# A 64 KB store of zeros on ScalarE's queue, beside the first load of a log-softmax backward kernel

## Chip, cores and metric

The kernel runs on one core of a Trainium2 chip. The metric is the device time of one execution in microseconds (us). Runs of one kernel mostly agree within 0.3%.

## The reference

```python
def reference(y, dy):                       # both (8, 1024, 8192) float32
    softmax_x = np.exp(y)
    sum_dy = np.sum(dy, axis=-1, keepdims=True)
    return (dy - softmax_x * sum_dy).astype(np.float32)
```

Two arrays of 268 MB are read and one is written: 805 MB for very little arithmetic.

## The kernel before

The 8192 rows are handled in 32 groups of 256; a partition holds two rows of a group side by side, 64 KB. VectorE sums dy (with the sign turned), ScalarE takes the exponential of y in place, VectorE computes `e * s + d` into the dy tile, and the dy tile is stored. All transfers are issued from one queue, SyncE's (SP).

```python
    def load_dy(g):
        dy_t = dyp.tile([P, R * D], fp32, name="dy_t")          # 2 buffers of 64 KB a partition
        nc.sync.dma_start(out=dy_t[:], in_=dy_v[g])             # line 45
        s_t = stats.tile([P, R], fp32, name="s_t")
        nc.vector.tensor_reduce(...)                            # line 47
        return dy_t, s_t

    def load_y(g): ...      # two loads of 32 KB rows, line 60
    def compute(...): ...   # line 69: nc.scalar.activation; line 70: nc.vector.scalar_tensor_tensor
    def store(g, dy_t, parts=1): ...                            # line 77, on nc.sync

    cur = load_dy(0)
    for g in range(G):                                          # G = 32
        if g < G - 1:
            y_ts = load_y(g)
            compute(*cur, y_ts)
            nxt = load_dy(g + 1)
            if g < G - 2:
                store(g, cur[0])
                cur = nxt
            else:
                held, cur = cur, nxt
        else:
            ...             # last group: its compute, the held store, then the last store in two parts
```

## Time and profile before

| | before |
|---|---|
| time, median of the three runs known at the start | 1871.92 us (1868.21 to 1875.18) |
| span of the profiled execution | 1865.4 us |
| busy: VectorE (DVE), ScalarE (ACT) | 60%, 25% |
| bytes moved, mean rate | 805 MB, 432 GB/s |

The next fence is from the page of the kernel before: the row of DMA busy tenths in 40 equal slices, and the queue table (queue, packets, MB, share of sixteen engines' span).

```profile
DMA  9999999999999999999999999999999999999999
...
q1 hardware_dynamic: 18576, 805.31, 99.9%
```

The DMA engines never rest and no compute engine comes near that, so the DMA engines set the time.

The timeline of the head of the kernel before has the start, the duration, engine (SPq is SP's queue of issues), line and operation, and in brackets the engine's idle time before it and what ended that.

```profile
0.73 0.38 SPq L45 DMA_DIRECT2D dy_t<-in_dy_dram  x1
1.17 0.90 SPq L60 DMA_DIRECT2D y_t<-in_y_dram  x2
2.11 0.53 SPq L45 DMA_DIRECT2D dy_t<-in_dy_dram  x1
22.74 17.22 DVE L47 TENSOR_REDUCE s_t<-dy_t 128x2 f32<-128x16384 f32 x1 [22.74 <-DMA dy_t<-in_dy_dram]
32.42 7.12 ACT L69 ACTIVATE y_t<-y_t 128x4096 f32<-128x4096 f32 x2 [30.42 <-DMA y_t<-in_y_dram]
...
57.77 0.35 SPq L77 DMA_DIRECT2D out_dram<-dy_t  x1
...
113.31 0.34 SPq L77 DMA_DIRECT2D out_dram<-dy_t  x1
```

The four loads issued in the first 2.64 us hold 25 MB, some 58 us of DMA work. VectorE has nothing to do until 22.74 us and ScalarE nothing but its table load until 32.42 us. The first store follows at 57.77 us, close to where the four loads end.

The wait view for SP's queue before (who waited for whom, total us, times, longest):

```profile
SPq L77 <- DVE dy_t L70: 985.9, 32, 35.0
SPq L45 <- DMA out_dram<-dy_t: 742.0, 30, 25.6
```

Stores wait for VectorE and dy loads wait for a store to free their buffer. Since the engines are busy anyway, these waits cost nothing as they stand.

### The profile page before, as it was taken

Reading aid. Unit: us, or ns where it says so; the run is one execution under the profiler, and the core shown is the slowest. Engines: PE = TensorE matmul, PEld = TensorE weight load, DVE = VectorE, ACT = ScalarE, POOL = GpSimd, SP = SyncE. Lnnn points to the kernel's source line nnn. Section 1 sums busy time; section 2 is a strip of 40 time slices with the busy share of each in tenths; the row PEclk is TensorE's granted clock in tenths of the full one; section 3 lists DMA queues with packets and bytes.
Section 4 is the critical chain, followed back from the end, with each engine's and each line's share of the span. In section 5 each row is a group of like instructions: output and inputs, shape, how many; then the busy total and the mean of one; then the engine's idle time right before and its main releaser. Section 6 shows DMA issues by size and latency. Waiting matters only on the chain.

```text
span 1865.4 us, 712 instructions
## 1 busy us (share of the span) xinstructions
DVE 1119.2 (60%) x160; ACT 457.1 (25%) x129; POOL 0.2 (0%) x4
## 2 busy tenths in 40 slices
DVE  5675555755557555575555755657656576565664
ACT  2123321233212332123321233212332113331132
POOL 0000000000000000000000000000000000000000
DMA  9999999999999999999999999999999999999999
GB/s 427 416 434 431 443 433 422 435 437 436 427 433 431 440 430 434 431 429 441 433 437 425 433 442 431 434 425 436 438 434 433 428 434 437 437 431 430 429 435 396
DMA packets 18582, 805.36 MB, mean 432 GB/s; under 512 B 2064, under 2 KB 2064, under 8 KB 2064
## 3 DMA queue, kind: packets, MB, share of 16 engines
q1 hardware_dynamic: 18576, 805.31, 99.9%
q14 instruction: 6, 0.05, 0.0%
HBM read 536.87 MB, written 268.44 MB: 432 GB/s over the span
## 4 chain that ended last, share of the span: by engine, by line
DMA 74%; DVE 17%; ACT 6%; SPq 1%; issue 1%; DVEq 0%; ACTq 0%
DMA y_t<-in_y_dram 69%; DVE dy_t L70 15%; ACT y_t L69 6%; DMA dy_t<-in_dy_dram 3%; DVE s_t L47 2%; DMA out_dram<-dy_t 1%; SPq L60 1%; SPq L77 1%; DVEq L122 0%; ACTq L69 0%; DVEq L70 0%
## 5 line engine op out<-in xcount | busy, mean ns | idle before, releaser
L70 DVE SCALAR_TENSOR_TENSOR dy_t<-y_t,s_t,dy_t 128x4096 f32<-128x4096 f32 x128 | 568.1, 4481 | 490.3 <-ACT y_t L69 490.1
L69 ACT ACTIVATE y_t<-y_t 128x4096 f32<-128x4096 f32 x128 | 455.9, 3608 | 1375.6 <-DMA y_t<-in_y_dram 1375.6
L47 DVE TENSOR_REDUCE s_t<-dy_t 128x2 f32<-128x16384 f32 x32 | 551.0, 17220 | 232.1 <-DMA dy_t<-in_dy_dram 232.1
L69 ACT ACT_TABLE_LOAD x1 | 1.3, 1283 | 0.7 <-PEq L111 0.7
L111 POOL MEMSET const-bfloat16-1.0<- 128x1 bf16 x1 | 0.1, 102 | 0.0
L111 POOL MEMSET const-uint8-127<- 128x1 uint8 x1 | 0.1, 102 | 0.0
L111 POOL MEMSET const-float32-1.0<- 128x1 f32 x1 | 0.1, 99 | 0.0
L111 POOL MEMSET const-float32-0.0<- 128x1 f32 x1 | 0.1, 98 | 0.2 <-issue 0.2
## 6 DMA issues: line engine op xcount, KB each, us to landing
y_t<-in_y_dram SPq DMA_DIRECT2D x64, 4096.0 KB, 35.9
out_dram<-dy_t SPq DMA_DIRECT2D x2, 4096.0 KB, 22.6
dy_t<-in_dy_dram SPq DMA_DIRECT2D x32, 38.7
out_dram<-dy_t SPq DMA_DIRECT2D x31, 26.1
```

The lines of the kernel that those rows point to most:

```text
L47: nc.vector.tensor_reduce(out=s_t[:], in_=dy_t[:].rearrange("p (r d) -> p r d", r=R), axis=mybir.AxisListType.X, op=ALU.add, negate=True,)
L60: nc.sync.dma_start(out=y_t[:], in_=y_v[g][:, r * D : (r + 1) * D])
L69: nc.scalar.activation(e, e, EXP)
L70: nc.vector.scalar_tensor_tensor(out=d, in0=e, scalar=s_t[:, r : r + 1], in1=d, op0=ALU.mult, op1=ALU.add)
L77: nc.sync.dma_start(out=out_v[g][:, k * w : (k + 1) * w], in_=dy_t[:, k * w : (k + 1) * w])
L111: nc = _bacc.Bacc("TRN2", target_bir_lowering=False, num_devices=1)
```

## The change

The change adds one store on a second queue before anything else. It writes zeros into rows of the last group's output, which the last group's own store overwrites at the end. No reason comes with it; what it does is to have a write, and a second queue, in use from the start.

```diff
+    first_t = stats.tile([P, 128], fp32, name="first_t")
+    nc.vector.memset(first_t[:], 0.0)                                   # line 83
+    nc.scalar.dma_start(out=out_v[G - 1][:, :128], in_=first_t[:])      # line 84
+
     cur = load_dy(0)
```

## The prediction

> **What bounds the kernel now.** The DMA engines. In the row of slices their busy share is 9 tenths or more in all 40; the queue table puts 805.31 MB and 99.9% of sixteen engines' span on the one hardware queue (SP's), at a mean of 432 GB/s over 1865.4 us. VectorE is busy 60%, ScalarE 25%. In the timeline ScalarE starts on two neighbouring late groups at 1719.50 and 1777.57, so a group takes 58.1 us; it moves 25.17 MB, which is 433 GB/s. The time is bytes over a rate that hardly moves (slices from 396 to 443 GB/s), plus about 1 us before the first bytes and about 3 us after most of the last ones (the windows view has 295 GB/s in 1860 to 1862 us, 49 in the next two).
>
> **What the change adds.** It removes nothing.
> - A memset of 128x128 on VectorE. The four small memsets in the trace take 0.1 us each; I estimate 0.1 to 0.2 us. VectorE is idle until 22.74 us (timeline): free.
> - One DMA issue on ScalarE, some 0.4 us as on SP (0.33 to 0.53 us), beside the table load at 0.72 to 2.00 us. ScalarE has nothing else to do before 32.42 us: free.
> - 64 KB on the DMA engines, in 128 rows of 512 B. By bytes at 432 GB/s that is 0.15 us. The rows are small: the Trainium skill, "DMA: Bandwidth & Descriptors", section "Measured", lists 0.95 us of engine time for a 64 KB transfer (a load by another path, so an estimate of the upper end). The trace before holds no such data packet, so it neither agrees nor disagrees.
> - Probably one more semaphore condition on the last group's first store and one more queue in the final drain, both met some 1800 us earlier: below 0.1 us.
>
> **How much is on the critical path.** Only the DMA engine time. By 2.64 us SP has issued the first dy load, both y loads and the second dy load, 25 MB or 58 us of work, so what the small store takes from the engines delays everything behind it and arrives whole at the end: 0.15 to 1 us, 0.3 us as my figure, 0.02% of the time. Less, if the store slips in before the first load's bytes flow. The small store may itself land late, even 20 us, if its rows take turns with the first load's 64 KB rows; nobody waits for it. The order of work on SP should stay, since no other transfer depends on the new one until the last group.
>
> The three runs before spread over 7 us (1868.21 to 1875.18), far more than the effect; that spread sets my range.
>
> **Predicted:** 1872.2 us, 1866.5 to 1878.5 eight times in ten. Faster by over 2%: 0.01; within 2%: 0.97; slower by over 2%: 0.02.
>
> **What would show the steps right or wrong.**
> - The queue table gains a second hardware queue with 65.5 KB and far below 0.1%; the first stays at 805.31 MB and 99.8 to 99.9%.
> - A group stays at 58.1 us; the slices stay at 9s with some 430 GB/s.
> - The first reduction starts at 22.7 us plus at most 1 us; the last store is issued at most 1 us later than 1841.6 us.
> - In the wait view no new wait longer than 1 us appears on SP, ScalarE or VectorE.
>
> **What would make it wrong.** An early write to the output that makes later transfers wait for one another (new waits on SP, gaps in the DMA row); a reordering of SP's instructions; or a DMA rate that changes once two queues have been in use (another group period through the whole run). A gain over 2% would need more than 440 GB/s sustained, which only single slices of the trace show.

## The result, and the profile after

| | before | after |
|---|---|---|
| median of 6 runs | 1868.88 us | 1868.38 us |
| lowest to highest | 1867.29 to 1875.18 | 1867.66 to 1871.71 |
| profiled span | 1865.4 us | 1866.1 us |

The ratio is 0.9993, 95% interval 0.9977 to 1.0010: the same. A ratio is the mean time of one kernel's fast runs over that of the other's fast runs of the same rounds, so it is not quite the ratio of the medians quoted.

From the page of the kernel after, the DMA row, the queue table, and the issue line of the new store (KB, us from issue to landing):

```profile
DMA  9999999999999999999999999999999999999999
...
q1 hardware_dynamic: 18576, 805.31, 99.9%
q10 hardware_dynamic: 144, 0.07, 0.0%
...
out_dram<-first_t ACTq DMA_DIRECT2D x1, 64.0 KB, 22.9
```

(ACTq is ScalarE's queue of issues.) The old queue is untouched and a second one has 128 rows and 16 completion records of 4 B, one for each DMA engine. But those 64 KB took 22.9 us to land, that is, from issue until all of it was reported as done.

The timeline of the head after, with lines 83 and 84 new:

```profile
0.73 0.38 SPq L45 DMA_DIRECT2D dy_t<-in_dy_dram  x1
0.82 0.17 DVE L83 MEMSET first_t<- 128x128 f32 x1 [0.82 <-PEq L116]
1.02 0.41 ACTq L84 DMA_DIRECT2D out_dram<-first_t  x1
...
22.70 17.22 DVE L47 TENSOR_REDUCE s_t<-dy_t 128x2 f32<-128x16384 f32 x1 [21.71 <-DMA dy_t<-in_dy_dram]
32.39 7.12 ACT L69 ACTIVATE y_t<-y_t 128x4096 f32<-128x4096 f32 x2 [29.65 <-DMA y_t<-in_y_dram]
...
57.72 0.35 SPq L77 DMA_DIRECT2D out_dram<-dy_t  x1
...
113.53 0.34 SPq L77 DMA_DIRECT2D out_dram<-dy_t  x1
```

Every line shown of before has its counterpart within 0.3 us. ScalarE's table load alone moved by more: it starts at 1.46 us, 0.72 before, behind the issue of the new store. SP's wait view after:

```profile
SPq L77 <- DVE dy_t L70: 985.3, 32, 35.0
SPq L45 <- DMA out_dram<-dy_t: 743.3, 30, 25.7
```

No new wait appears on SP. ScalarE's wait view has one, that of its table load:

```profile
ACT L69 <- DVE first_t L83: 1.5, 1, 1.5
```

The trace also keeps each packet of the DMA engines. This is an excerpt of the records after (time since the first load's first packet, queue, bytes, duration), the sixteen engines mixed:

```
  3.491 q1    65536 B  2420 ns
  3.525 q1    65536 B  2418 ns
  5.404 q10     512 B    27 ns
  5.428 q1    65536 B  2418 ns
  5.449 q10     512 B    27 ns
  5.472 q1    65536 B  2418 ns
```

Each engine puts one 512 B row between two 64 KB rows and no more; one such place of the small row is called a turn here. The start of one round of 64 KB rows to the next is 2.415 us before (median start of the rounds 3.32 and 17.81 us, six rounds apart) and 2.438 us after (3.31 and 17.94 us). So one turn costs 23 ns, the eight turns that an engine owes cost some 0.2 us, and the store is finished only after eight of those rounds: each engine's first six small rows stand between 64 KB rows, the seventh after its last one, and the eighth behind the 4 B completion record of that load. That is my theory of the result: the store costs its turns, 0.2 us, and its late landing is harmless while nobody waits for it. The Trainium skill says of this, in "DMA: Bandwidth & Descriptors", section "Queues, rings and completion order", that an engine "round-robins between the queue rows it has work for, at *packet* granularity"; the records above agree, with one record, here one row, to a turn.

### The profile page after: what moved, and what is told of

It reads as the page before. It is cut to its first block, busy times and chain, and to the rows that moved or that the text cites. A ratio compares the mean times of both kernels' runs of the same rounds, so it can differ in the third digit from the quotient of the medians.

```text
span 1866.1 us, 714 instructions
## 1 busy us (share of the span) xinstructions
DVE 1119.4 (60%) x161; ACT 457.1 (24%) x129; POOL 0.2 (0%) x4
## 3 DMA queue, kind: packets, MB, share of 16 engines
q1 hardware_dynamic: 18576, 805.31, 99.9%
## 4 chain that ended last, share of the span: by engine, by line
DMA 74%; DVE 17%; ACT 6%; SPq 1%; issue 1%; DVEq 0%; ACTq 0%
DMA y_t<-in_y_dram 69%; DVE dy_t L70 15%; ACT y_t L69 6%; DMA dy_t<-in_dy_dram 3%; DVE s_t L47 2%; DMA out_dram<-dy_t 1%; SPq L60 1%; SPq L77 1%; DVEq L127 0%; ACTq L69 0%; DVEq L70 0%
## 6 DMA issues: line engine op xcount, KB each, us to landing
out_dram<-first_t ACTq DMA_DIRECT2D x1, 64.0 KB, 22.9
```

## The experiments

All kernels gave the right result. The edits are against the changed kernel, except in the two experiments that start from the kernel with small rows; "..." marks lines left out.

### The change again, and a null

The first repeats the changed kernel and the second is the kernel before against itself, five rounds each.

> The changed kernel once more, in five rounds. My theory: the store costs only its turns on the DMA engines, 8 rows of 27 ns per engine in the trace, 0.22 us, so the ratio to the kernel before is 1.0001 and no run of this length can see it: 0.999 to 1.001. Rival: opening a second hardware queue, or an early write, slows something for good; then the ratio is above 1.001 in every round.

> The kernel before against itself, five rounds: what a ratio of no change looks like here. Expected within 0.999 to 1.001, as wide as for the changed kernel.

| | median | ratio to before | 95% |
|---|---|---|---|
| change again | 1868.24 us | 0.9992 | 0.9978 to 1.0007 |
| before against itself | 1869.84 us | 1.0001 | 0.9985 to 1.0017 |

The null has an interval as wide as the change's, and both hold 1; the rival's 1.001 lies above that of the change (1.0007). An effect of 0.2 us (0.01%) can't be seen in time here; it must be made larger. The expected width of 0.1% was a little too narrow.

### The store 32 times larger, in small rows

```diff
-    nc.scalar.dma_start(out=out_v[G - 1][:, :128], in_=first_t[:])
+    nc.scalar.dma_start(
+        out=out_v[G - 1][:, :8192].rearrange("p (k c) -> p k c", c=256)[:, :, :128],
+        in_=first_t[:].unsqueeze(1).to_broadcast([P, 32, 128]),
+    )
```

> The store made 32 times larger in the same 512 B rows (2.10 MB, 256 rows per engine), one DMA. Turns theory: 256 x 27 ns = 6.9 us more engine time, all of it in the span: +6 to +9 us, ratio 1.003 to 1.005. The store takes one turn per row of the SP queue, 32 rows per engine in a group of 58 us, so it lands only after some 465 us. No new wait on SP. Rival 1 (bytes alone count): 2.10 MB at 432 GB/s, +4.9 us. Rival 2 (it hides in the head): +0 to 1 us, landing within some 30 us.

The median was 1878.06 us against 1868.92, ratio 1.0048 (1.0027 to 1.0069), so some +9 us. Landing and a wait were not as expected. The issue line of the early store, from this kernel's page:

```profile
out_dram<-first_t ACTq DMA_DIRECT2D x1, 2048.0 KB, 125.5
```

SP's wait view of this kernel:

```profile
SPq L77 <- DVE dy_t L70: 953.0, 31, 35.0
...
SPq L77 <- DMA out_dram<-first_t: 42.8, 1, 42.8
```

And from its timeline, VectorE's last work on the second group and that group's store:

```profile
106.45 8.88 DVE L70 SCALAR_TENSOR_TENSOR dy_t<-y_t,s_t,dy_t 128x4096 f32<-128x4096 f32 x2 [0.99 <-ACT y_t L69]
...
126.57 0.34 SPq L77 DMA_DIRECT2D out_dram<-dy_t  x1
```

The turns go as expected at first: by the packet records 32 rows an engine by 58 us. Then the second group's store, whose data are ready at 106.45 + 8.88 = 115.3 us, is held until 126.57 us, although it writes other rows (the 42.8 us count from SP's issue before; 11.2 of them come after the data are ready). SP's queue runs dry, and the other 187 rows of each engine flow back to back in 4.4 us, one every 23.5 ns; then the engines stand still for 1.3 us, until the first row of the next store. So the cost is some 6.0 us (from start to start) to 6.9 us (256 x 27 ns) of rows and 1.3 us of idle time, 7 to 8 of the 9 us. The rest is within the noise: the large rows alone took 1863.1 us of each engine in the profiled run before and 1868.1 us in that of the null. Hiding in the head (0 to 1 us) is far outside the interval (5.0 to 12.9 us). Bytes alone (4.9 us) is just outside, but inside once the 1.3 us of idle time are added; what speaks against it is the 6.0 to 6.9 us of the records.

Why it waits shows in the compiled program's listing of SP's instructions, here from the changed kernel (second column: line in the kernel):

```
8  L77 DMACopy out_dram<-dy_t 128x16384 [waits DMAHW4_49,DMAHW1_49,DVE_49]     after
8  L77 DMACopy out_dram<-dy_t 128x16384 [waits DMAHW3_49,DVE_49]               before
```

The listing itself is not kept with the runs, but the trace of the changed kernel agrees: the early store and the second group's store both raise semaphore 101, and SP waits for that one ahead of the latter. The program has eight completion counters for transfers (in the trace, semaphores 100 to 103 and 105 to 108), taken in turn. The early store has counter 1, and the transfer eight places later, the second group's store, shares it and so waits for it. That condition is in the changed kernel too: it is met at 23.9 us, some 90 us before the store that asks for it.

### The same bytes in 8 KB rows

```diff
-    first_t = stats.tile([P, 128], fp32, name="first_t")
+    first_t = stats.tile([P, 2048], fp32, name="first_t", bufs=1)
...
-    nc.scalar.dma_start(out=out_v[G - 1][:, :128], in_=first_t[:])
+    nc.scalar.dma_start(
+        out=out_v[G - 1][:, :8192].rearrange("p (k c) -> p k c", c=4096)[:, :, :2048],
+        in_=first_t[:].unsqueeze(1).to_broadcast([P, 2, 2048]),
+    )
```

> The same 2.10 MB in 8 KB rows (16 per engine), one DMA. Turns theory: some 0.30 us a row, 16 x 0.30 = 4.9 us more engine time and as much in the span, ratio 1.0026, about 2 us less than with the small rows; 16 turns behind eight 64 KB rows and eight 32 KB rows, so landing at some 35 us, thirteen times earlier than the small rows. Rival (cost is per byte and landing per byte): same time and same landing as with the small rows.

The median was 1873.95 us, against the same 1868.92: ratio 1.0020 (1.0003 to 1.0037), 3.7 us by the ratio and 5.0 by the medians. The store's issue line, from this kernel's page:

```profile
out_dram<-first_t ACTq DMA_DIRECT2D x1, 2048.0 KB, 35.8
```

The first reduction, from its timeline:

```profile
25.47 17.22 DVE L47 TENSOR_REDUCE s_t<-dy_t 128x2 f32<-128x16384 f32 x1 [22.48 <-DMA dy_t<-in_dy_dram]
```

It landed after 35.8 us, as the count of turns said, and its 8 KB rows took 309 ns each, 16 x 0.309 = 4.9 us an engine. The first reduction moved from 22.70 to 25.47 us, most of which is the seven turns taken ahead of the first load's completion records (7 x 0.309 = 2.2 us). Same bytes, another landing: landing goes by rows, cost by the time of the rows. For the cost that rests on the packet records, since the two intervals overlap.

### Small rows to the first group

```diff
-        out=out_v[G - 1][:, :8192].rearrange("p (k c) -> p k c", c=256)[:, :, :128],
+        out=out_v[0][:, :8192].rearrange("p (k c) -> p k c", c=256)[:, :, :128],
```

> The 2.10 MB in 512 B rows again, but to rows of the first group, whose real store is wanted at 57.7 us. Theory (the late landing was harmless only because nobody waits for it): now SP waits at its first store. By then 24 to 32 of 256 turns per engine are taken; the SP queue runs dry at about 60 us, and then the other 224 rows flow at 27 ns each, 6 us. So a new SP wait of some 8 to 10 us, the first store is issued at 66 to 69 us, landing at about 66 us, not 465, and the span is 2 to 6 us longer than with the same rows in the last group (+9 to +13 us against before). Rival (landing never matters, the engines are busy with something anyway): the same time as with the last group's rows.

The median was 1877.69 us, against 1869.55: ratio 1.0052 (1.0023 to 1.0081). From SP's wait view of this kernel:

```profile
SPq L77 <- DMA out_dram<-first_t: 65.2, 1, 65.2
```

And the first group's store, from its timeline:

```profile
68.05 0.35 SPq L77 DMA_DIRECT2D out_dram<-dy_t  x1
```

The first store moved from 57.72 to 68.05 us, as expected (the 65.2 us count from SP's issue before; VectorE is done at 58.0 us, so some 10 of them are new). But the time is that of the last group's rows, since those made a store wait too. The comparison of the two therefore decided nothing; what it shows is that a late landing is felt once someone waits for it. The records have the same 1.3 us in which all engines stand still, here at 67.6 us.

### Another partner on the counter

To tell the shared counter from a check of overlapping rows, the small-rows kernel got two more transfers between the early store and the second group.

```diff
-            nc.sync.dma_start(out=y_t[:], in_=y_v[g][:, r * D : (r + 1) * D])
+            h = D // 2 if g == 0 else D
+            for c in range(0, D, h):
+                nc.sync.dma_start(
+                    out=y_t[:, c : c + h], in_=y_v[g][:, r * D + c : r * D + c + h]
+                )
```

> The store of 2.10 MB in 512 B rows to the last group's rows again. In its first run SP's store of the second group waited 42.8 us for it, though their rows do not overlap. Theory (the compiled program reuses eight completion counters in turn, and the transfer eight places after the early store on the list waits for it): with the first group's y loads cut into two pieces each, two transfers more stand in between, so the waiting one is now the second y load of the second group, a load, which has nothing to do with the output. Expected: no wait of a store for the early store; instead a wait of a y load (line 62) of some 35 us, landing at some 95 us in place of 125, span again +8 to +10 us. Rival (a check of overlapping output rows makes the stores wait): the second group's store waits again, landing at some 125 us.

SP's waits in this kernel (line 62 is the y load, line 81 the store):

```profile
SPq L81 <- DVE dy_t L74: 977.7, 32, 35.0
...
SPq L62 <- DMA out_dram<-first_t: 38.5, 1, 38.5
```

The store of the second group no longer waits. A load of y, which touches no output, waits 38.5 us for a store of zeros, and the store lands after 96.1 us. The shared counter is the reason, not the rows. The time was 1879.82 us against 1868.23, ratio 1.0061 (1.0046 to 1.0076): +11 us where 8 to 10 were expected, of which 8.6 to 10 lies within the interval (8.6 to 14.2 us).

### The first load in 16 KB rows

```diff
-        nc.sync.dma_start(out=dy_t[:], in_=dy_v[g])
+        for k in range(4 if g == 0 else 1):
+            w = R * D // (4 if g == 0 else 1)
+            nc.sync.dma_start(
+                out=dy_t[:, k * w : (k + 1) * w], in_=dy_v[g][:, k * w : (k + 1) * w]
+            )
```

> The store as in the change, on ScalarE's queue, but the first load cut into four loads of 16 KB rows. Turns theory: the store's 8 rows per engine stand each behind a row of 0.6 us instead of 2.4 us, so it lands about 6 to 9 us after issue instead of 22.9. Rival (fixed cost of the second queue or of the write): landing stays at 20 us or more. Time unchanged within 0.3%.

The store's issue line, from this kernel's page:

```profile
out_dram<-first_t ACTq DMA_DIRECT2D x1, 64.0 KB, 9.7
```

The same store on the same queue to the same rows landed after 9.7 us, not 22.9 (a little over the 6 to 9 expected). So what it stands behind, not the queue's first use or the first write, sets when it lands. One run, state unknown: 1867.71 us.

### The store on SP's queue: reordered, then truly first

The first attempt only changed the queue.

```diff
-    nc.scalar.dma_start(out=out_v[G - 1][:, :128], in_=first_t[:])
+    nc.sync.dma_start(out=out_v[G - 1][:, :128], in_=first_t[:])
```

> The 64 KB store on SP's own queue, ahead of the first load. Turns theory: no big rows to take turns with, so landing some 2 us after its issue, not 22.9. SP waits for the memset and then issues the store for 0.4 us, so the first load is issued at about 1.4 us, not 0.73, and everything behind it, first reduction and end, moves by 0.6 to 0.9 us; in time still within the spread, ratio 0.999 to 1.001. Rival (the 22.9 us belong to a first write to this memory, or to a queue's first use): landing stays at some 20 us.

The start of this kernel's timeline:

```profile
0.73 0.37 SPq L45 DMA_DIRECT2D dy_t<-in_dy_dram  x1
...
1.16 0.42 SPq L84 DMA_DIRECT2D out_dram<-first_t  x1
```

The scheduler of the program had put the store, which waits for the memset, behind the first load. It then landed 21.7 us after issue, behind that load's 64 KB rows in one queue, and the test told nothing about the rival (ratio 0.9995, 0.9976 to 1.0014). The second attempt forces the order:

```diff
-    nc.scalar.dma_start(out=out_v[G - 1][:, :128], in_=first_t[:])
+    first = nc.sync.dma_start(out=out_v[G - 1][:, :128], in_=first_t[:])
...
-    cur = load_dy(0)
+    with tc.issue_after(first.ins):
+        cur = load_dy(0)
+        y_first = load_y(0)
...
-            y_ts = load_y(g)
+            y_ts = load_y(g) if g else y_first
```

> The 64 KB store on SP's queue, this time really first (the run before it was reordered behind the first load). Turns theory: no 64 KB rows to stand behind, landing some 2 to 3 us after issue; the first load is issued at about 1.5 us in place of 0.73, and the first reduction moves from 22.7 to some 23.5 us; span +0.5 to +1 us, ratio 0.999 to 1.002. Rival (the 22.9 us belong to a first write or a first use of the queue): landing some 20 us after issue.

The store's issue line, from this kernel's page:

```profile
out_dram<-first_t SPq DMA_DIRECT2D x1, 64.0 KB, 1.6
```

The first load and the first reduction, from its timeline:

```profile
1.43 0.42 SPq L45 DMA_DIRECT2D dy_t<-in_dy_dram  x1
...
23.61 17.22 DVE L47 TENSOR_REDUCE s_t<-dy_t 128x2 f32<-128x16384 f32 x1 [22.62 <-DMA dy_t<-in_dy_dram]
```

Alone in front, the same 64 KB lands in 1.6 us, and the first reduction moves by 0.9 us, 0.7 us of it because the first load is issued that much later. The ratio is 1.0009 (0.9994 to 1.0024), which can't tell 0.7 us from nothing. The turns of a second queue (0.2 us in all) are cheaper than an issue ahead of the first load (0.7 us), by the trace.

### VectorE's work ahead of the loop

Two attempts repeated the small memset 96 and 196 times.

```diff
-    nc.vector.memset(first_t[:], 0.0)
+    for _ in range(96):      # 196 in the second kernel
+        nc.vector.memset(first_t[:], 0.0)
```

> The memset repeated 96 times, some 16 us of VectorE in place of 0.17, the store behind them. My theory: VectorE is idle until the first load has landed at 22.7 us, so all of it is free: first reduction still at 22.7 us, ratio 0.999 to 1.001. Rival (VectorE's work ahead of the loop always adds up): +16 us, ratio 1.0085.

> The memset repeated 196 times, some 32 to 33 us of VectorE. Now it ends about 10.5 us after the first load has landed. The first store then moves from 57.7 to about 68 us, while the queue of the four first loads ends at about 60 us: the DMA engines stand idle for some 9 us, so the span grows by 8 to 11 us, ratio 1.004 to 1.006. Rival (the DMA rate alone sets the time, VectorE has slack everywhere): no change.

The medians were 1870.02 us (ratio 0.9999, 0.9979 to 1.0019) and 1875.61 us (1.0028, 1.0008 to 1.0048), against 1869.02. Neither is the test that was meant: the scheduler spread the memsets between the loop's instructions. From the second kernel's timeline:

```profile
0.83 23.67 DVE L84 MEMSET first_t<- 128x128 f32 x92 [0.83 <-PEq L117]
...
24.41 17.16 DVE L47 TENSOR_REDUCE s_t<-dy_t 128x2 f32<-128x16384 f32 x1
...
61.44 11.27 DVE L84 MEMSET first_t<- 128x128 f32 x44
61.49 0.35 SPq L77 DMA_DIRECT2D out_dram<-dy_t  x1
```

92 of them went ahead of the reduction at 257 ns each, not 165; in the first kernel too, whose reduction also started at 24.41 us and not at the 22.7 expected. The third attempt holds ten larger memsets ahead of it:

```diff
-    first_t = stats.tile([P, 128], fp32, name="first_t")
-    nc.vector.memset(first_t[:], 0.0)
-    nc.scalar.dma_start(out=out_v[G - 1][:, :128], in_=first_t[:])
+    first_t = stats.tile([P, 2048], fp32, name="first_t", bufs=1)
+    for _ in range(10):
+        last = nc.vector.memset(first_t[:], 0.0)
+    nc.scalar.dma_start(out=out_v[G - 1][:, :128], in_=first_t[:, :128])
...
-    cur = load_dy(0)
+    with tc.issue_after(last.ins):
+        cur = load_dy(0)
```

> Ten memsets of 128x2048, some 1.8 us each, all held ahead of the first reduction: 18 to 20 us of VectorE that end before the first load has landed; the store follows them. Theory (VectorE's time before 22.7 us is free): first reduction at 22.7 to 23 us, first store at 57.7 to 58 us, ratio 0.999 to 1.001. Rival (work ahead of the loop adds up): +18 us, ratio 1.0095.

From this kernel's timeline, the last memset, the first reduction and the first store:

```profile
21.55 1.76 DVE L84 MEMSET first_t<- 128x2048 f32 x1 [0.49 <-DVE first_t L84]
23.23 17.16 DVE L47 TENSOR_REDUCE s_t<-dy_t 128x2 f32<-128x16384 f32 x1
...
58.20 0.35 SPq L77 DMA_DIRECT2D out_dram<-dy_t  x1
```

The memsets, 0.49 us apart, filled VectorE until 23.3 us, half a microsecond past the landing of the first load, and the first store moved from 57.72 to 58.20 us. The ratio is 1.0016 (1.0000 to 1.0033): 3 us by the ratio, by 2.6 us in the medians, but only 1.6 us between the profiled spans (1867.0 and 1865.4 before). The rival's 18 us are ruled out; by time alone, whether the cost is 0, 0.5 or 3 us is left open. The packet records say more: between the first load's first packet and 140 us, the sixteen engines stood idle for 0.2 us on average in the kernel before and in this one, so in the profiled run the later store cost nothing. In the second kernel they stood idle for 5.2 us, as much as its +5 us (by its ratio), mostly where its late stores left SP's queue dry. So VectorE's time after the first load has landed was not free there, though its memsets lay in several places.

## Why the prediction was right, point by point

- **The time** (1872.2 us, 1866.5 to 1878.5, within 2%) held: 1868.38 us. The figure leaned on three runs before with a median of 1871.92 us; with three more it is 1868.88, which explains 3.0 of the 3.8 us.
- **DMA engines bound the kernel**: right. Work put on them appears in the time: 2.1 MB in 8 KB rows cost 3.7 to 5.0 us, for 4.9 us of engine time. In 512 B rows it cost 9 us, 6 to 7 of it rows and 1.3 idle time.
- **"0.15 to 1 us, 0.3 us as my figure"**: the term was 0.2 us by the records (8 turns of 23 to 27 ns on each engine). The 0.95 us of the skill's table is for a load by another path, and was far above. In the time of the change itself it can't be seen.
- **"The small store may itself land late, even 20 us"**: it landed after 22.9 us, and the reason given was right: one row a turn behind 64 KB rows. With 16 KB rows in the way it took 9.7 us, with none 1.6 us.
- **"Nobody waits for it", "no other transfer depends on the new one until the last group"**: this step was wrong, though it did not matter at 64 KB. A transfer of the second group waits for the early store, because they share a completion counter. The slack is some 90 us, not the 1800 us of the text. With 2.1 MB in small rows the slack was gone: the store was held for 11 us after its data were ready.
- **Free memset and issue**: the trace has 0.17 us on VectorE at 0.82 us and 0.41 us on ScalarE's queue at 1.02 us, and nothing behind them moved but the table load. That VectorE has room for far more until the first load lands is shown by the last memset run: 22 us of memsets added no idle time to the DMA engines in its profile, while its time only says at most some 6 us (ratio up to 1.0033).
- **The signs named**: the second queue with 0.07 MB and 0.0%, the first with 99.9%, the first reduction at 22.70 us, a group of 58.1 us (late reductions at 1749.11 and 1807.17 us), the last store issued at 1842.2 us instead of 1841.6 (within the 1 us allowed), and no new wait over 1 us on SP came as written. One did not: ScalarE's wait view names a new wait of 1.5 us, the table load behind the new store (0.7 us before). It ended 30 us before ScalarE was needed.

No version was clearly faster than these two kernels; with the engines at 99.9% of the span there was none to be expected from moving this store.

## What to carry to other kernels

In a kernel that the DMA engines bind, as here, cost a small extra transfer by its rows times the time of a row on each engine, and expect it to land after as many turns as it has rows on an engine, each as long as one row of the queue beside it, as long as that queue has work. Before calling a late landing harmless, look for who waits for it, and not only by the data: completion counters are shared by transfers that have no data in common, so an early slow transfer can hold an unrelated load. And check the order in the compiled program before an experiment runs: three of these twelve did not test what they were written for.

## What the Trainium skill lacked or had wrong

- "DMA: Bandwidth & Descriptors", section "Queues, rings and completion order", gives about 9 to 17 descriptors as typical of one turn. Here a turn was one packet record, which held one row (how many descriptors a row has the trace does not say): eight 512 B rows an engine took eight turns, six of them between 64 KB rows and two behind the last, 22.9 us in all against 1.6 us alone.
- The same page, section "Measured", lists 0.95 us for 64 KB by another path and direction and has no row for a store like this one. The store here, from ScalarE's queue, took 8 x 27 ns = 0.22 us of each engine; alone on SP's queue its rows lay within 0.36 us.
- The same page, section "Specifications", names 512 B as the least transfer for full rate. Back to back, 512 B rows of a store started 23.5 ns apart, 16 x 512 B / 23.5 ns = 349 GB/s; 64 KB rows took 2.418 us, 434 GB/s; 8 KB rows 309 ns, 424 GB/s.
- No page that I read says that a compiled program shares eight completion counters among all its transfers on both queues, so that a transfer can wait for an unrelated one eight places before it: 38.5 us for a load that had no data in common with it.
